# One level of Strassen's algorithm in the first feed-forward product of a fused encoder layer

## The chip, the core and the metric

The kernel runs as one program on one core of a Trainium2 chip. TensorE (PE) multiplies matrices into PSUM banks; VectorE (DVE), ScalarE (ACT) and GpSimd (POOL) work elementwise; SyncE (SP) issues this kernel's DMAs. Each engine works through its own list of instructions in order, and an instruction may wait for semaphores that other engines and the DMAs raise. The metric is the time of one execution in microseconds (us) on the device.

## The reference

One layer for 2048 prompt tokens and 8 x 16 tokens of running streams, 2176 in all, model width 1024, in float32. Cut to what matters here:

```
h = rms_norm(x, norm_mix_w) * (1 + sc1) + sh1
u, z, xbc, dt = split(h @ w_in)              # input projection
ya = pool_mixer(u); yb = ssd_mixer(z, xbc, dt)
x = x + g1 * (concat(ya, yb) @ w_out)        # output projection
h = rms_norm(x, norm_ffn_w) * (1 + sc2) + sh2
f = square(relu(h @ w_ff1 + b_ff1)) @ w_ff2 + b_ff2   # 1024 -> 4096 -> 1024
x = x + g2 * f
y = rms_norm(x, final_norm_w)
```

The two feed-forward products, `h @ w_ff1` and `(...) @ w_ff2`, are equally large. The shift, scale and gate vectors (sh, sc, g) are one set for the prompt and one for each of the 8 streams.

## The kernel before, in words

**Numbers.** Activations lie transposed: 128 features on the partitions, tokens along the free axis. To keep float32 precision every operand is split into a high part (a cast to `fp32r`) and a low part (the value minus the high part). `mm3` (L173) multiplies high by high, high by low and low by high: three matmuls for each 128x128 weight tile (a k-tile), added in one PSUM bank. `wsplit` (L163) loads 512 KB of weights into `wr`, makes the high part `wh` on ScalarE (L168) and the low part `wl` on VectorE (L170).

**Blocks and phases.** The tokens are cut into five blocks of 384 and one of 256 (`TBS`; the last holds the 128 tokens of the running streams). Blocks are worked on in three pairs (`SUPERS`), so that each weight tile serves two blocks. Phase A (input projection and the two mixers) comes first, then phase O (`out_proj`, L814), then the feed-forward (L968 to L982). Between phases, results go through DRAM: `yD` and `pD` hold the mixers' outputs, `xD` the stream after the output projection. The last write of `yD` is at L640, by a DMA on SyncE's queue.

**Feed-forward.** `load_r` (L838) reads a pair's `xD` tiles, keeps them as the residual input `xs`, and sums their squares for the norm. `load_h` (L860) scales them by the norm's factor and the modulation (`modulate`) and splits them: 2 blocks x 8 k-tiles, each with two instructions on VectorE and two on ScalarE. `ff1` (L881) makes four weight tiles of 128 outputs at a time: for each tile and block 8 k-tiles, so 24 matmuls, into one PSUM bank; then ReLU (L895) and the square's high part (L896) on ScalarE, the square (L897) and its low part (L898) on VectorE. `ff2` (L902) multiplies these by the second weights, 12 matmuls for each output tile, and adds the result to `xs` (L913). Per pair, `ff1` and `ff2` alternate eight times, with `ff1` one step ahead. The last `ff2` of a pair sums squares, normalizes and writes the output (L943).

**What sets the order.** Each engine's list is drawn up when the kernel is built, from the order of the program text, moved by `tc.high_priority(offset=...)`, and by when buffers come free: a tile of a pool with a fixed number of buffers waits for the last user of its buffer. Side work (the loading of the next inputs) is kept in a list of steps, `fill`; `filler(n)` takes n of them at chosen places, `drain()` takes all. Large activations lie in three classes of buffers, `c0`, `c1` and `c2` (`qt`), of 32 tiles each; a class passes from one phase's use to the next's. PSUM gives four banks `g`, two `y` and two `t`; `obank` deals out `g` and `y` in turn.

## Time and profile before

| | |
|---|---|
| Median of three runs | 2984.9 us (2980.18 to 2986.68) |
| Span of the profiled execution | 2982.6 us |
| TensorE busy | 2920.5 us, 98% |
| VectorE busy | 1812.6 us, 61% |
| ScalarE busy | 1170.2 us, 39% |
| GpSimd busy | 0.2 us |
| Read from and written to DRAM | 292.53 MB and 49.08 MB, 115 GB/s over the span |

The span runs from the first instruction to the last of one execution that the hardware profiler took. A busy time is the time in which at least one instruction of the engine was under way. A matmul's own duration in the profile is longer than the distance from its start to the next one's start, since matmuls overlap; where TensorE is never idle, the length of a stretch divided by its number of matmuls is the time that one takes up.

### The profile page before, as it was taken

The page shows a single profiled execution, that of the slowest core. Times are in us where ns is not written, and L with a number is a line of the kernel's source. Part 1 is how long each engine was busy: PE and PEld are TensorE (multiplying, and loading weights), DVE is VectorE, ACT ScalarE, POOL GpSimd, SP SyncE. Part 2 cuts the span into 40 slices and gives each one's busy share as a digit, 9 for nine tenths or more (in the row PEclk, how much of TensorE's full clock was granted, in tenths as well). Part 3 has the DMA queues.
Part 4 walks back from the last instruction along what each step waited for, and adds up shares of the span by engine and source line. Part 5 has one row for each costly group of instructions (what it writes and reads, how often), then busy time and mean ns, then how long its engine had stood idle before and what let it go on. Part 6 is the DMA issues. An engine that isn't in the chain of part 4 may idle for free.

```text
span 2982.6 us, 44472 instructions
## 1 busy us (share of the span) xinstructions
PE 2920.5 (98%) x17572; PEld 2822.1 (95%) x17572; DVE 1812.6 (61%) x3592; ACT 1170.2 (39%) x2098; POOL 0.2 (0%) x4
## 2 busy tenths in 40 slices
PE   7999999999999999999999999999999999999998
PEld 5889998989989899999999999999999999999997
DVE  8588796778978684543644444674444458445546
ACT  7646455544624233232622222542222234332232
POOL 0000000000000000000000000000000000000000
PEclk8999999999999999999999999999999999999999
DMA  6657343523564565563111111141111113222122
GB/s 233 195 181 218 130 127 111 149 91 114 160 166 150 157 204 168 144 220 123 62 64 64 64 64 64 63 163 64 64 64 64 57 64 135 75 75 78 71 78 78
DMA packets 218433, 344.51 MB, mean 116 GB/s; under 512 B 48816, under 2 KB 163440, under 8 KB 218224
## 3 DMA queue, kind: packets, MB, share of 16 engines
q1 hardware_dynamic: 218224, 341.67, 35.9%
q8 instruction: 138, 2.26, 0.3%
q14 instruction: 71, 0.58, 0.1%
HBM read 292.53 MB, written 49.08 MB: 115 GB/s over the span
## 4 chain that ended last, share of the span: by engine, by line
PE 90%; DVE 4%; DMA 4%; ACT 1%; issue 1%; SPq 0%; DVEq 0%; ACTq 0%
PE g L174 20%; PE g L175 20%; PE g L176 20%; PE y L176 7%; PE y L175 7%; PE y L174 7%; PE y L591 1%; PE t L596 1%; PE y L589 1%; DMA sb<-h 1%; PE t L254 1%; PE t L231 1%; DMA E<-aD 1%; PE g L211 1%; DMA EA<-aD 1%
## 5 line engine op out<-in xcount | busy, mean ns | idle before, releaser
L174 PE MATMUL g<-h,wh 128*128 128x384 f32 (+1 forms) x2584 | 856.5, 332 | 7.2 <-ACT h L785 3.5
L176 PE MATMUL g<-h,wl 128*128 128x384 f32 (+1 forms) x2584 | 857.8, 332 | 0.0
L175 PE MATMUL g<-h,wh 128*128 128x384 f32 (+1 forms) x2584 | 855.4, 331 | 0.0
L168 ACT CAST wh<-wr 128x1024 fp32r<-128x1024 f32 x386 | 403.1, 1050 | 987.7 <-PE g L175 740.8
L170 DVE TENSOR_TENSOR wl<-wr,wh 128x1024 fp32r<-128x1024 f32 x386 | 470.9, 1224 | 361.6 <-ACT wh L168 352.0
L174 PEld LDWEIGHTS g<-h,wh 128*128 128x128 f32 x2584 | 489.7, 190 | 19.2 <-issue 7.8
L175 PEld LDWEIGHTS g<-h,wh 128*128 128x128 f32 x2584 | 489.6, 189 | 9.5 <-issue 6.8
L176 PEld LDWEIGHTS g<-h,wl 128*128 128x128 f32 x2584 | 489.7, 190 | 8.7 <-issue 5.9
L174 PE MATMUL g<-c,wh 128*128 128x384 f32 (+1 forms) x1300 | 428.8, 330 | 1.4 <-ACT c L785 1.4
L176 PE MATMUL g<-c,wl 128*128 128x384 f32 (+1 forms) x1300 | 428.6, 330 | 0.0
L175 PE MATMUL g<-c,wh 128*128 128x384 f32 (+1 forms) x1300 | 428.1, 329 | 0.0
L913 DVE SCALAR_TENSOR_TENSOR c<-g,mod,c 128x384 f32<-128x384 f32 (+1 forms) x261 | 150.3, 576 | 199.2 <-PE g L176 198.8
L174 PEld LDWEIGHTS g<-c,wh 128*128 128x128 f32 x1300 | 244.3, 188 | 2.9 <-ACT c L785 2.2
L175 PEld LDWEIGHTS g<-c,wh 128*128 128x128 f32 x1300 | 244.2, 188 | 0.4
L176 PEld LDWEIGHTS g<-c,wl 128*128 128x128 f32 x1300 | 244.1, 188 | 0.4
L897 DVE TENSOR_TENSOR m<-m 128x384 f32<-128x384 f32 x192 | 102.3, 533 | 211.5 <-ACT c L896 211.5
L176 PE MATMUL y<-h,wl 128*128 128x384 f32 (+1 forms) x680 | 223.7, 329 | 0.0
L175 PE MATMUL y<-h,wh 128*128 128x384 f32 (+1 forms) x680 | 223.7, 329 | 0.0
L174 PE MATMUL y<-h,wh 128*128 128x384 f32 (+1 forms) x680 | 223.6, 329 | 0.0
L175 PE MATMUL y<-c,wh 128*128 128x384 f32 (+1 forms) x620 | 202.8, 327 | 0.0
L176 PE MATMUL y<-c,wl 128*128 128x384 f32 (+1 forms) x620 | 202.8, 327 | 0.0
L174 PE MATMUL y<-c,wh 128*128 128x384 f32 (+1 forms) x620 | 202.7, 327 | 0.0
(219 smaller groups left out, 3529.6 us busy)
## 6 DMA issues: line engine op xcount, KB each, us to landing
wr<-wf SPq DMA_DIRECT2D x204, 512.0 KB, 3.5
wr<-win SPq DMA_DIRECT2D x84, 512.0 KB, 4.2
wr<-wada SPq DMA_DIRECT2D x48, 512.0 KB, 5.0
E<-aD SPq DMA_DIRECT2D x34, 512.0 KB, 5.6
x<-xT SPq DMA_DIRECT2D x88, 192.0 KB, 3.1
wr<-wob SPq DMA_DIRECT2D x24, 512.0 KB, 3.9
wr<-wcD SPq DMA_DIRECT2D x24, 512.0 KB, 3.5
x<-uD SPq DMA_DIRECT2D x40, 199.5 KB, 3.3
```

The costliest lines, as they stand in the source:

```text
L168: S.copy(wh, raw)
L170: V.tensor_tensor(wl, raw, wh.bitcast(F32), op=ALU.subtract)
L174: T_.matmul(out, lhsT=wh, rhs=ah, start=start, stop=False)
L175: T_.matmul(out, lhsT=wh, rhs=al, start=False, stop=False)
L176: T_.matmul(out, lhsT=wl, rhs=ah, start=False, stop=stop)
L211: T_.matmul(out, lhsT=csh[i][:, k, :], rhs=wh[:, k2 * 512:(k2 + 1) * 512], start=(i + k == 0), stop=False)
L231: T_.matmul(pn[:, c:c + 1], lhsT=acc[:, c * P:(c + 1) * P], rhs=ones[:, 0:1], start=True, stop=True)
L254: T_.matmul(pr[:, :T], lhsT=ones, rhs=dg[:, :T], start=True, stop=True)
L589: T_.matmul(pO[:, pr, :], lhsT=St[g][:, pr * P:(pr + 1) * P], rhs=Cg, start=True, stop=True)
L591: T_.matmul(pD[64 * (h % 2):64 * (h % 2) + 64, h // 2, :], lhsT=xdt[:, h, :], rhs=M[:, h, :], start=True, stop=True)
L897: V.tensor_tensor(t, t, t, op=ALU.mult)
L913: V.scalar_tensor_tensor(x1[:, :Tp], pg[:, :Tp], G[:, 0:1], x1[:, :Tp], op0=ALU.mult, op1=ALU.add)
```

## The change

**The product.** `ff1` gives way to `ff1_unit`. A unit takes two weight tiles of 128 outputs (m0 = 2u, m1 = 2u + 1), the two halves of the contraction (512 each) and the pair's two token blocks, and sees them as a 2 x 2 by 2 x 2 product of blocks. One level of Strassen's algorithm, in Winograd's form, makes it with 7 block products in place of 8: each is 4 k-tiles, so 12 matmuls, and a pair has 16 units. Three of the four PSUM banks (`pa`, `pc`, `pb`) take a second product on top of the first (`more=True`): what the first left is read before, or counts in the sum. Further sums of results are made by VectorE on the way out (L995 to L997, L1004, L1006) in tiles `e` of a new pool `fe` with six buffers. `put` then makes ReLU, square and high part on ScalarE in three instructions and the low part on VectorE.

**Operands.** Strassen's products need four sums of weight blocks (s1 to s4) and four sums of activations (t1 to t4). The weight sums are made once for all pairs by GpSimd, in `combine`, 32 times (16 units, two halves): two DMAs bring 256 KB each into the single buffer `pp`, four additions of 128 x 256 follow, and a DMA writes 512 KB to a scratch `sD[u]` in DRAM; all three DMAs are issued by GpSimd. `combine` is called after the loads of the first pair's mixer outputs and ahead of the first `out_proj`. `wpair` then loads pairs of 512-column pieces, from the weights or from `sD`, and splits them. The activation sums are made by VectorE in `load_h`, which now reads the `xD` tiles itself through staging tiles, scales them (`affine`) and gives seven operands for each quarter: b11, t3 and t1 in class `c2`, t2, b21, t4 and b22 in `c1`. `load_x` reads the residual input again.

**Blocks and order.** The feed-forward's blocks become four of 364 and two of 360 tokens (`FBS`), since both blocks of a pair must be equally wide; the columns sum to 2176 in both. `xcols` gathers a block of 364 or 360 from the `xD` blocks of 384. `rsqrt_diag` takes widths that are no multiple of 128. `ff2(i)` needs the units 2i and 2i + 1 and runs after unit 2i + 2; the last two follow unit 15. The pool `pp` is closed ahead of the feed-forward, and `fe` takes over its memory. Cut from the diff below are changes of comments, the passing on of arguments, and the functions told in words.

```diff
+FBS = [364, 364, 364, 364, 360, 360]
...
     def rsqrt_diag(tp, acc, T, scale, epsval):
-        n = T // P
+        n = -(-T // P)
+        if T < n * P:
+            V.memset(acc[:, T:n * P], 1.0)
...
+    def affine(t, xk, r, dim, Ac, Bc):
+        T, _, last, Tp = dim
         V.tensor_tensor(t, xk, r[:, :T], op=ALU.mult)
         S.activation(t[:, :Tp], t[:, :Tp], AF.Identity, scale=Ac[:, 0:1], bias=Bc[:, 0:1])
...
+    sD = [dr.tile([P, 4, 512], F32, name=f"sD{u}") for u in range(16)]
+
+    def combine(pool, u, half):
+        hs = slice(256 * half, 256 * half + 256)
+        w = pool.tile([P, 4, 256], F32, tag="pp", name="pp", bufs=1)
+        for i in range(2):
+            nc.gpsimd.dma_start(w[:, 2 * i:2 * i + 2], a["wf1"][2 * u + i].rearrange("p (b x) -> p b x", b=2)[:, :, hs])
+        for out, x, y, op in ((3, 2, 3, ALU.add), (2, 0, 2, ALU.subtract), (0, 3, 0, ALU.subtract), (1, 1, 0, ALU.subtract)):
+            nc.gpsimd.tensor_tensor(w[:, out], w[:, x], w[:, y], op=op)
+        nc.gpsimd.dma_start(sD[u][:, :, hs], w)
+
+    def xcols(dst, k, t0, T):
+        for s, (lo, n) in enumerate(zip(OFFS, TBS)):
+            b, e = max(t0, lo), min(t0 + T, lo + n)
+            if b < e:
+                DQ.dma_start(dst[:, b - t0:e - t0], xD[s][k][:, b - lo:e - lo])
...
+    def load_h(sup, rs):
+        T = FBS[sup[0]]
+        hs = {n: [None] * 4 for n in HOPS}
+
+        def put(n, q, raw):
+            cls = "c2" if n in ("b11", "t3", "t1") else "c1"
+            hi, lo = qt(cls, F32R), qt(cls, F32R)
+            S.copy(hi[:, :T], raw)
+            V.tensor_tensor(lo[:, :T], raw, hi[:, :T].bitcast(F32), op=ALU.subtract)
+            hs[n][q] = (hi, lo)
...
+        def one(q):
+            b11, b12, b21, b22 = raws(q)
+            put("b11", q, b11)
+            t1 = tmp()[:, :T]
+            V.tensor_tensor(t1, b12, b11, op=ALU.subtract)
+            V.tensor_tensor(b12, b22, b12, op=ALU.subtract)
+            put("t3", q, b12)
+            put("t1", q, t1)
+            V.tensor_tensor(t1, b22, t1, op=ALU.subtract)
+            put("t2", q, t1)
+            put("b21", q, b21)
+            V.tensor_tensor(t1, b21, t1, op=ALU.subtract)
+            put("t4", q, t1)
+            put("b22", q, b22)
...
-    def ff1(sup, hs, i, cls):
...
+    def ff1_unit(sup, hs, u, cls):
...
+        def put(j, q, c):
+            fh, fl = qt(cls, F32R), qt(cls, F32R)
+            S.activation(c, c, AF.Relu)
+            S.activation(c, c, AF.Square)
+            S.copy(fh[:, :T], c)
+            V.tensor_tensor(fl[:, :T], c, fh[:, :T].bitcast(F32), op=ALU.subtract)
+            f[j][q] = (fh, fl)
...
+        pa, pc, pb, pd = (bank(ps, "g", GB) for _ in range(4))
+        wa11, ws3 = wpair(a11, s3_)
+        prod(pa, wa11, "b11")
+        c11 = ev()
+        S.activation(c11, pa[:, :T], AF.Identity, bias=VC("bf1", m0))
+        prod(pc, ws3, "t3")
+        ws1, ws2 = wpair(s1, s2)
+        prod(pb, ws1, "t1")
+        prod(pa, ws2, "t2", True)
+        u2 = ev()
+        S.copy(u2, pa[:, :T])
+        wa12, wa22 = wpair(a12, a22)
+        prod(pd, wa12, "b21")
+        v = ev()
+        V.tensor_tensor(v, u2, pc[:, :T], op=ALU.add)
+        V.scalar_tensor_tensor(v, pb[:, :T], VC("bf1", m1), v, op0=ALU.add, op1=ALU.add)
+        V.tensor_tensor(c11, c11, pd[:, :T], op=ALU.add)
+        prod(pc, wa22, "t4", True)
+        ws4, = wpair(s4)
+        prod(pb, ws4, "b22", True)
+        put(0, 0, c11)
+        put(1, 1, v)
+        c21 = ev()
+        V.scalar_tensor_tensor(c21, pc[:, :T], VC("bf1", m1), u2, op0=ALU.add, op1=ALU.add)
+        put(0, 1, c21)
+        V.scalar_tensor_tensor(u2, pb[:, :T], VC("bf1", m0), u2, op0=ALU.add, op1=ALU.add)
+        put(1, 0, u2)
...
+    pstack = ExitStack()
+    pp = pstack.enter_context(tc.tile_pool(name="pp", bufs=1))
+    for u in range(16):
+        for half in range(2):
+            combine(pp, u, half)
     pin1 = in_pool(SUPERS[1], "c2")
...
     with tc.high_priority(offset=FPRIO):
-        filler(16)
+        drain()
+    pstack.close()
+    fe = region("fe")
...
+        for u in range(16):
+            f[u] = ff1_unit(sup, hs, u, "c1" if u == 15 else "c0")
+            if u >= 2 and u % 2 == 0 and u < 14 or u == 15:
+                for i in ([u // 2 - 1] if u < 15 else [6, 7]):
...
+                    ff2(sup, xs, i, fi, i == 7)
```

**What moves.** On GpSimd nothing ran before but a few settings at the program's start. Now its list goes on with the rounds of `combine`. The names in brackets are the semaphores waited for: DMAHW are the DMA queues of SyncE, DMASW those of GpSimd, the rest are engines.

```order
L857 DMA pp<-wf 128x2x256 [waits DMAHW3_49,DMAHW2_49,DMAHW4_49,DMAHW1_49,DMAHW5_49,DMAHW0_49,DMAHW6_49,DVE_49,DMAHW7_49,PE_49,Activation_49]
L857 DMA pp<-wf 128x2x256
L859 ISA
L859 TENSOR_TENSOR pp<-pp 128x256 [waits DMASW1_49]
L859 TENSOR_TENSOR pp<-pp 128x256 [waits DMASW0_49,Pool_49]
L859 TENSOR_TENSOR pp<-pp 128x256 [waits Pool_49] x2
L860 DMA sD_10895<-pp 512x1x256 [waits Pool_49]
L857 DMA pp<-wf 128x2x256 [waits DMASW2_49]
```

The first load waits for all that has gone before on the other engines and SyncE's queues; the load of the second round waits for the write of the first.

On ScalarE at the start of the feed-forward, before (L286, L290 and L873 are `load_h`, L895 and L896 the first evictions of `ff1`, L168 a weight split):

```order
L290 CAST h<-m 128x384 [waits Activation_49]
L873 ACTIVATE c_13717<-c_13717,g2b 128x384
L290 CAST h<-m 128x384 [waits Activation_49]
L286 ACTIVATE m<-m,mod,A_89 128x384 [waits DVE_49]
L895 ACTIVATE m<-g,vec 128x384 [waits DVE_49,PE_49]
L290 CAST h<-m 128x384 [waits Activation_49]
L896 ACTIVATE c_14933<-m 128x384 [waits Activation_49]
L873 ACTIVATE c_13718<-c_13718,g2b 128x384
L873 ACTIVATE c_13719<-c_13719,g2b 128x384
L168 CAST wh<-wr 128x1024 [waits DMAHW7_49,PE_49]
```

The same place after (L295 and L899 are `load_h`, L985 is the first unit's first eviction into a tile `e`):

```order
L295 ACTIVATE x<-x,mod,A_89 128x364 [waits DVE_49,Activation_49]
L899 CAST c_15233<-x 128x364 [waits DVE_49]
L899 CAST c_15237<-m 128x364
L899 CAST c_15277<-x 128x364 [waits Activation_49]
L295 ACTIVATE x<-x,mod,A_89 128x364 [waits DMAHW7_49,DMAHW0_49,DVE_49]
L985 ACTIVATE e<-g,vec 128x364 [waits DMASW3_49,DMASW4_49,DMASW2_49,DMASW5_49,DMASW1_49,DMASW6_49,DMASW0_49,DMASW7_49,PE_49,Pool_49]
L899 CAST h<-m 128x364 [waits DVE_49]
L295 ACTIVATE x<-x,mod,A_89 128x364 [waits DVE_49]
L899 CAST h<-x 128x364
```

The first eviction now names every DMA queue of GpSimd and GpSimd itself among its waits, and the rest of `load_h` stands behind it.

On VectorE in the middle of the first pair, before (L897 and L898 belong to `ff1`, L913 to `ff2`):

```order
L170 TENSOR_TENSOR wl<-wr,wh 128x1024
L897 TENSOR_TENSOR m<-m 128x384
L898 TENSOR_TENSOR c_15770<-m,c_15769 128x384
L897 TENSOR_TENSOR m<-m 128x384
L898 TENSOR_TENSOR c_15764<-m,c_15763 128x384
L170 TENSOR_TENSOR wl<-wr,wh 128x1024
L897 TENSOR_TENSOR m<-m 128x384
L913 SCALAR_TENSOR_TENSOR c_13711<-g,mod,c_13711 128x384
L898 TENSOR_TENSOR c_15772<-m,c_15771 128x384
L913 SCALAR_TENSOR_TENSOR c_13719<-y,mod,c_13719 128x384
L913 SCALAR_TENSOR_TENSOR c_13712<-g,mod,c_13712 128x384
L913 SCALAR_TENSOR_TENSOR c_13720<-g,mod,c_13720 128x384
```

The same work after, in one unit (L954 is `wpair`, L995 to L997, L1004 and L1006 the sums of results, L975 the low parts):

```order
L954 TENSOR_TENSOR wl<-wr,wh 128x1024
L954 TENSOR_TENSOR wl<-wr,wh 128x512
L954 TENSOR_TENSOR wl<-wr,wh 128x1024
L995 TENSOR_TENSOR e<-e,g 128x364
L997 TENSOR_TENSOR e<-e,g 128x364
L996 SCALAR_TENSOR_TENSOR e<-g,vec,e 128x364
L1004 SCALAR_TENSOR_TENSOR e<-g,vec,e 128x364
L975 TENSOR_TENSOR c_17288<-e,c_17287 128x364
L954 TENSOR_TENSOR wl<-wr,wh 128x1024
L1006 SCALAR_TENSOR_TENSOR e<-g,vec,e 128x364
L975 TENSOR_TENSOR c_17294<-e,c_17293 128x364
L954 TENSOR_TENSOR wl<-wr,wh 128x1024
```

Between two weight splits there were up to four short instructions; in a unit the sums of results and the low parts come together in its second half, with weight splits among them.

## Rows read from the trace of the kernel before

**Rows 1.** The page: span, busy time by engine, the chain by engine.
```profile
span 2982.6 us, 44472 instructions
...
PE 2920.5 (98%) x17572; PEld 2822.1 (95%) x17572; DVE 1812.6 (61%) x3592; ACT 1170.2 (39%) x2098; POOL 0.2 (0%) x4
...
PE 90%; DVE 4%; DMA 4%; ACT 1%; issue 1%; SPq 0%; DVEq 0%; ACTq 0%
```

**Rows 2.** Busy time by stretch (x: instructions), then granted clock, DMA share, GB/s.
```profile
core 0: us, PE busy (x) PEld busy (x) DVE busy (x) ACT busy (x) POOL busy (x), PEclk, DMA share, GB/s
1052.00:1424.00 372.00, 370.12 (x2237) 368.24 (x2235) 189.79 (x364) 123.11 (x199) 0.00 (x0) 1.00 0.54 168
1424.00:1452.00 28.00, 25.07 (x131) 23.92 (x132) 24.06 (x51) 26.89 (x53) 0.00 (x0) 0.94 0.15 52
1500.00:1800.00 300.00, 300.00 (x1718) 300.00 (x1717) 125.56 (x180) 71.72 (x100) 0.00 (x0) 1.00 0.18 63
2550.00:2850.00 300.00, 300.00 (x2042) 300.00 (x2041) 151.08 (x293) 87.30 (x134) 0.00 (x0) 1.00 0.22 76
1875.00:1955.00 80.00, 80.00 (x460) 79.74 (x459) 55.40 (x93) 47.92 (x82) 0.00 (x0) 1.00 0.22 76
```

**Rows 3.** SyncE's queue in time order, 1046 to 1049 us: start, duration, issue.
```profile
1048.17 0.37 SPq L640 DMA_DIRECT2D yD<-zz  x1
```

**Rows 4.** ScalarE in time order, 1423.5 to 1424.5 us.
```profile
1424.00 0.45 ACT L830 ACTIVATE m<-y,g1b,mod 128x128 f32<-128x128 f32 x1
```

**Rows 5.** VectorE's groups by form: count, busy us, mean ns, idle before.
```profile
L170 DVE TENSOR_TENSOR wl<-wr,wh 128x1024 fp32r<-128x1024 f32 x386 | 470.9, 1224 | 361.6 <-ACT wh L168 352.0 <-PE g L212 3.0 <-DMA wr<-wada 1.4
L913 DVE SCALAR_TENSOR_TENSOR c<-g,mod,c 128x384 f32<-128x384 f32 x221 | 136.3, 617 | 171.2 <-PE g L176 170.8
L897 DVE TENSOR_TENSOR m<-m 128x384 f32<-128x384 f32 x160 | 88.9, 556 | 211.5 <-ACT c L896 211.5
...
L897 DVE TENSOR_TENSOR m<-m 128x256 f32<-128x256 f32 x32 | 13.4, 419 | 0.0
```

**Rows 6.** DMA issues: count, KB each, median us from issue to landing.
```profile
wr<-wf SPq DMA_DIRECT2D x204, 512.0 KB, 3.5
...
E<-aD SPq DMA_DIRECT2D x34, 512.0 KB, 5.6
...
yD<-zz SPq DMA_DIRECT2D x10, 768.0 KB, 4.1
...
zz<-xT SPq DMA_DIRECT2D x2, 768.0 KB, 8.4
```

**Rows 7.** VectorE's largest group by form from 1052 to 1424 us.
```profile
L170 DVE TENSOR_TENSOR wl<-wr,wh 128x1024 fp32r<-128x1024 f32 x46 | 56.3, 1224 | 79.0 <-ACT wh L168 79.0
```

**Rows 8.** ScalarE's groups by form.
```profile
L168 ACT CAST wh<-wr 128x1024 fp32r<-128x1024 f32 x386 | 403.1, 1050 | 987.7 <-PE g L175 740.8 <-PE y L175 232.5 <-PE g L211 8.1
L896 ACT ACTIVATE c<-m 128x384 fp32r<-128x384 f32 x160 | 84.2, 526 | 4.7
L895 ACT ACTIVATE m<-g,vec 128x384 f32<-128x384 f32 x99 | 57.2, 578 | 112.6 <-PE g L176 112.6
...
L290 ACT CAST h<-m 128x384 fp32r<-128x384 f32 x40 | 20.0, 499 | 0.0
```

**Rows 9.** VectorE in time order, 2975 to 2983 us.
```profile
2975.95 3.22 DVE L943 SCALAR_TENSOR_TENSOR c<-c,vec,t 128x256 f32<-128x256 f32 x8 [1.38 <-PE t L254]
```

More of the change, by code (lines that the diff above doesn't have):

```diff
@@ L31 @@
 TM = max(TBS)
+FBS = [364, 364, 364, 364, 360, 360]
+FOFFS = [sum(FBS[:i]) for i in range(len(FBS))]
+FLAST = len(FBS) - 1
+FLP = FBS[FLAST] - NB * DS
 _V = {}
@@ L171, in wsplit, with mm3 @@
         return wh, wl
-    def mm3(out, wh, wl, ah, al, start, stop):
-        T_.matmul(out, lhsT=wh, rhs=ah, start=start, stop=False)
-        T_.matmul(out, lhsT=wh, rhs=al, start=False, stop=False)
-        T_.matmul(out, lhsT=wl, rhs=ah, start=False, stop=stop)
+    def mm3(out, wh, wl, ah, al, start, stop, more=False):
+        T_.matmul(out, lhsT=wh, rhs=ah, start=start, stop=False, skip_group_check=more)
+        T_.matmul(out, lhsT=wh, rhs=al, start=False, stop=False, skip_group_check=more)
+        T_.matmul(out, lhsT=wl, rhs=ah, start=False, stop=stop, skip_group_check=more)
     csw = ca.tile([P, KT, 192], F32R, name="cs")
@@ L276, in s3, with fdims @@
         return ap.rearrange("p (b i) -> p b i", b=NB)
+    def fdims(s):
+        T = FBS[s]
+        return T, FOFFS[s], s == FLAST, (FLP if s == FLAST else T)
     def dims(s):
@@ new lines, in load_x, with wpair @@
+        return xs
+    def wpair(*srcs):
+        n = 512 * len(srcs)
+        with tc.high_priority(offset=WPRIO):
+            raw = wp.tile([P, 1024], F32, tag="wr", name="wr", bufs=WRB)
+            for i, src in enumerate(srcs):
+                DQ.dma_start(raw[:, 512 * i:512 * i + 512], src)
+            wh = wp.tile([P, 1024], F32R, tag="wh", name="wh")
+            S.copy(wh[:, :n], raw[:, :n])
+            wl = wp.tile([P, 1024], F32R, tag="wl", name="wl")
+            V.tensor_tensor(wl[:, :n], raw[:, :n], wh[:, :n].bitcast(F32), op=ALU.subtract)
+        return [(wh[:, 512 * i:512 * i + 512], wl[:, 512 * i:512 * i + 512]) for i in range(len(srcs))]
@@ new lines, in ff1_unit, with prod, ev @@
+    def ff1_unit(sup, hs, u, cls):
+        T = FBS[sup[0]]
+        m0, m1 = 2 * u, 2 * u + 1
+        def prod(out, w, n, more=False):
+            for q in range(4):
+                sl = slice(q * P, (q + 1) * P)
+                hi, lo = hs[n][q]
+                mm3(out[:, :T], w[0][:, sl], w[1][:, sl], hi[:, :T], lo[:, :T], q == 0 and not more, q == 3, more)
+        def ev():
+            return fe.tile([P, TM], F32, tag="e", name="e", bufs=6)[:, :T]
+        def put(j, q, c):
[5 more added lines that the diff above has]
+            f[j][q] = (fh, fl)
+        f = [[None] * 2 for _ in sup]
+        s2, s4, s3_, s1 = (sD[u][:, i] for i in range(4))
+        a11, a12, a22 = a["wf1"][m0][:, 0:512], a["wf1"][m0][:, 512:], a["wf1"][m1][:, 512:]
+        pa, pc, pb, pd = (bank(ps, "g", GB) for _ in range(4))
[25 more added lines that the diff above has]
+        put(1, 0, u2)
@@ L905, in tile_m @@
             mm = m % 2
-            T, t0, last, Tp = dims(s)
+            T, t0, last, Tp = fdims(s)
             x1 = xs[j][m]
```

100 lines of the change are left out of this document (43 added, 57 removed).

## The prediction

> **What bounds the kernel now.** I read the page's busy shares and chain first. TensorE (PE) is busy 98% of 2982.6 us and carries 90% of the chain; GpSimd (POOL) has 4 instructions in all [rows 1]. The reader is to see that only TensorE's time counts, unless another engine makes it wait. The table by stretches says how tightly. From 1500 to 1800 us, feed-forward on blocks of 384, TensorE is never idle, at full granted clock (2.4 GHz), with 1718 matmuls: 300/1718 = 174.6 ns each. From 2550 to 2850 us, blocks of 384 and 256 in equal number, 2042 matmuls take 146.9 ns each, so one of 256 columns takes 2 x 146.9 - 174.6 = 119.2 ns [rows 2]. The difference, 55.4 ns over 128 columns, is 0.433 ns a column. VectorE is busy 42% and ScalarE 24% of the first of these stretches. The groups by form and the DMA list then give the price of what is added.
>
> **The product itself.** The first product runs, for a pair of blocks, 32 weight tiles x 2 blocks x 24 matmuls = 1536; the change runs 16 units x 7 products x 12 = 1344. The second stays at 1536. By the slope a matmul of 364 columns takes 174.6 - 20 x 0.433 = 165.9 ns, one of 360 takes 164.2. Before: 1536 x (5 x 174.6 + 119.2) = 1524 us for the three pairs, both products. After: 1344 x (165.9 + 165.9 + 164.2) = 667 us and 1536 x 496.0 = 762 us, together 1429. **Saved: 95 us.** All of it is on the path. The new block widths alone change nothing: the columns sum to 2176 in both.
>
> **The GpSimd chain, the term that decides.** GpSimd forms the four weight sums of each unit: 32 times two DMAs in (512 KB together), four dependent additions of 128x256, one DMA out (512 KB). There is one buffer, so each round starts when the last one's output has landed. By the order the first waits for the last write of yD in the SSD phase, issued at 1048.2 us [rows 3], with 4 us to land: 1052. The end is awaited too: the pool "e" of the first eviction takes the chain's place in memory, and by the order that eviction, on ScalarE, waits for GpSimd's last rounds. Behind it on ScalarE stand the remaining third of load_h and the next weight casts, so TensorE runs dry within a few products.
>
> When would that eviction be ready otherwise? The output projection's last eviction starts on ScalarE at 1424.0 [rows 4]. In the order 58 VectorE instructions of load_h follow, 36 of them ahead of this eviction. At 0.42 us (256 columns) to 0.556 us (384) each [rows 5] the 58 take 24 to 32 us, I take 28; 36 of them make 17, so 1442. The chain has 390 us, 12.2 us a round.
>
> The trace has no GpSimd addition and no DMA issued by it, so a round is bounded by the nearest rows. Below: 3.5 us to load 512 KB, four additions at VectorE's 0.42 for 256 columns, and 4.1 us for the write of 768 KB [rows 5, 6]: 9.3 us. Above: 8.4 us, the slowest large load, each way [rows 6], and four additions at VectorE's 1.22 for 1024 columns [rows 5]: 21.7 us. I take 12.5: 4.6 in (midway between the 3.5 and the 5.6 of two loads of 512 KB, whose memory rows are longer and shorter than the 1 KB here), 4.5 out (a little over 4.1, as other transfers run beside it) and 0.85 an addition (midway between 0.42 and 1.22). Then 32 rounds make 400 us, the chain ends at 1452, **10 us late**. Every us on a round is 32 us.
>
> VectorE is busy 190 of the 372 us in which the chain runs, 56 of it in weight splits, which read two tiles of on-chip memory [rows 2, 7]. The Trainium skill (SBUF — State Buffer, Who interferes with whom) says that a VectorE instruction with two SBUF inputs and a GpSimd instruction that reads SBUF lock each other out, the second waiting for the whole of the first. By that rule each addition waits part of a VectorE instruction about every second time, an estimate of 0.2 us, near 1 us a round; no row of before can show it. The skill's DMA: Bandwidth & Descriptors (Anatomy of one DMA — SWDGE path) gives about 2.0 us plus bytes at 436 GB/s for a DMA from GpSimd: 3.2 us for 512 KB each way, an estimate of 9.8 us a round with my additions, by which the chain would be in time and the sum 10 us better. The two pull apart; the sum goes by the rows.
>
> **The start of the feed-forward.** Before, load_h needed two VectorE instructions a tile; now a quarter of the contraction needs 15 (4 scalings, 4 differences, 7 low parts). Half its tiles share the class c1 with the output projection's inputs, so by the order nearly all of it stands behind the projection's end. In these 28 us the order gives TensorE about 60 matmuls of the first unit, 10 us of work: 18 us idle. Before, 131 matmuls ran in the 28 us from 1424, where 28/0.1746 = 160 fit: 5 us lost, with the clock at 0.94 [rows 2]. I add 2 us for a lower clock after the longer gap. **Cost 15 us**, between 5 and 25.
>
> **Inside a unit.** At the end of the fourth product (t2) ScalarE may cast the next unit's first weights (1.05 us), then VectorE subtracts (1.22 us) [rows 5, 8]: 2.27 us. TensorE needs them after 12 + 2 matmuls, 2.32 us. Nothing is spare; I take 0.15 us for each of 48 units, **7 us** (0 to 30). The banks suffice: by the order each is evicted a product or more before it is needed again. Load does not bind in the mean: two units and one second product last 59 us on TensorE, against which ScalarE has 28 casts and activations at about 0.5 us and 11 weight tiles at 1.05 (26 us), VectorE 34 evictions and subtractions at about 0.55 and 11 tiles at 1.22 (32 us) [rows 5, 8].
>
> **Between the pairs.** While the last unit and the last two second products run (78 us of TensorE), VectorE has load_h (60 instructions), 32 evictions, 12 weight tiles, 14 additions of squares and the unit's own work: by durations 32 + 20 + 15 + 8 + 9 = 84 us, by the spacing when they follow each other some 70. Before, the same place had 55 of 80 us [rows 2]. I take 5 us for each of two such places, **10 us** (0 to 30).
>
> **Rest.** The output projection runs beside the chain's 33 MB, 84 GB/s on top of 168; the DMA share would rise from 0.54 to 0.81 [rows 2]. TensorE is busy 370 of 372 us there, covered by weights and inputs loaded ahead; if that cover thins, transfers at the two changes of input are late: 3 us (0 to 15). The last block is 360 wide, not 256: the eight closing multiplications took 3.22 us [rows 9], now about 4.5, with four shorter steps 2 us (1 to 4).
>
> **Sum.** 95 - 10 - 15 - 7 - 10 - 3 - 2 = 48 us. The profiled execution has a span of 2982.6 us; the median of the runs is 2984.9, so 2.3 lie around it, which I leave. 2984.9 - 48 = **2937 us**.
>
> **Rivals.**
> The first ends on the other side: the chain is much later. Mechanism: GpSimd's rounds, each with a full wait for two transfers and the additions held up beside a busy VectorE. With all else as above 58 us are gained without it, so it decides from 1442 + 58 = 1500 on, which is (1500 - 1052)/32 = 14.0 us a round. At 15 us a round the time is 2984.9 - 58 + 90 = 3017 us, at 17 us 3081. For it: nothing hides a round, the DMA share is high, and VectorE is half busy. Against it: the nearest rows make 9.3 us.
> The second: everything is hidden. The chain is in time (12 us or less) and the start, the units and the pairs cost half: 95 - 8 - 4 - 5 - 4 = 74, so 2911 us. For it: VectorE idles more than half of the steady stretch. Against it: the order puts load_h behind the projection's end.
> The third: the units bind. ScalarE and VectorE serve TensorE in order, four banks are all taken, and each unit loses 0.7 us more: 48 x 0.7 = 34, so about 2970 us. For it: the 2.27 against 2.32 us; against it: the second product between units lets queues catch up.
> The fourth: the change does not do what it says, as matmuls of 364 columns take the time of 384. Then FF takes 3 x (1344 + 1536) x 0.1746 = 1509 us, only 15 are saved and the time is about 3017 us. The straight line between 256 and 384 columns speaks against it.
>
> **How the numbers follow.** The forecast (chain up to 35 us late, others near their values): 0.50. Second rival 0.13, third 0.10, first 0.24, fourth 0.03. Faster by over 0.2% (about 6 us, what a measurement here can tell from no change): forecast, second and third, less 0.03 for those near the line, 0.70; slower 0.26, taking one hundredth of the first as even; within 0.2%: 0.04. The range reaches from 2903, below the second rival, to 3012, a round of 14.8 us. The forecast's own range is 2915 to 2965.
>
> **What would show it.** Right: 3 x (1536 - 1344) = 576 fewer matmuls, those of 364 columns spaced 166 ns; GpSimd's last addition near 1445 to 1455 us and TensorE idle for some 25 us around 1425 to 1460. Wrong: rounds longer than 14 us, so that ScalarE's first "e" waits for GpSimd beyond 1500; idle TensorE of more than half a microsecond in each unit, released by VectorE's wl or by evictions; a spacing of 364 columns above 170 ns.

## The result, and the profile after

The changed kernel takes 3002.4 us (median of five runs, 2994.8 to 3009.0) against 2982.9 us of the kernel before (five runs): a ratio of 1.0064, interval 1.0047 to 1.0082. It is slower by about 19 us where 48 us less were forecast. What came is in the main the first rival: the chain of weight sums ended at 1513.7 us, past the 1500 from which that rival decides. The profiled execution is the slowest of the five.

The page of the changed kernel, the lines that answer to [rows 1]:

```profile
span 3007.2 us, 45269 instructions
...
PE 2859.1 (95%) x17000; PEld 2742.3 (91%) x17000; DVE 1969.7 (65%) x3832; ACT 1348.3 (45%) x2518; POOL 184.2 (6%) x228
...
PE 73%; DMA 9%; issue 6%; POOL 5%; DVE 4%; ACT 2%; SPq 0%; DVEq 0%; POOLq 0%; ACTq 0%
```

TensorE has 572 matmuls and 61 us of work less than before, but its idle time grew from 62 to 148 us, and the chain that ended last now runs 9% through DMAs and 5% through GpSimd. The busy times by stretch, columns as in [rows 2]:

```profile
core 0: us, PE busy (x) PEld busy (x) DVE busy (x) ACT busy (x) POOL busy (x), PEclk, DMA share, GB/s
1424.00:1515.00 91.00, 21.59 (x97) 17.63 (x96) 27.79 (x48) 22.93 (x43) 37.34 (x49) 0.56 0.46 147
1515.00:1560.00 45.00, 41.99 (x219) 39.34 (x218) 31.96 (x55) 35.92 (x73) 0.00 (x0) 0.91 0.66 193
1600.00:1850.00 250.00, 250.00 (x1495) 247.78 (x1494) 136.46 (x215) 104.19 (x183) 0.00 (x0) 1.00 0.31 101
2600.00:2900.00 300.00, 300.00 (x1817) 297.68 (x1817) 170.95 (x314) 118.70 (x204) 0.00 (x0) 1.00 0.29 97
1930.00:2050.00 120.00, 113.41 (x656) 111.09 (x656) 99.53 (x191) 75.54 (x142) 0.00 (x0) 0.97 0.58 180
```

The third and fourth rows are the steady feed-forward: TensorE never idle, 167.2 ns a matmul on blocks of 364 (250/1495) and 165.1 with 360 (300/1817). The first two are where the time went: in 91 us after the output projection TensorE works for 21.6, at a mean granted clock of 0.56 (mostly the lower level, 1.2 GHz), and 45 us more pass before it is back at full pace. What it waited for from 1424 us on (total, times, longest):

```profile
PE g L178 <- ACT e L985: 47.6, 1, 47.6
PE g L178 <- ACT c L899: 15.9, 3, 8.8
```

One wait of 47.6 us, and its releaser is the first eviction of `ff1_unit`. On ScalarE, where [rows 4] stood, in time order:

```profile
1464.62 0.69 ACT L295 ACTIVATE x<-x,mod,A 128x364 f32<-128x364 f32 x1 [0.26 <-DVE x L294]
1513.78 0.56 ACT L985 ACTIVATE e<-g,vec 128x364 f32<-128x364 f32 x1 [48.47 <-DMA sD<-pp]
```

ScalarE was free at 1465.2, when the instruction ahead of the eviction was done, and TensorE's last matmul ahead of the gap started at 1466.3; the eviction started at 1513.8. So up to 48.5 us went to a write of `sD` that has nothing to do with the eviction but the memory. GpSimd in time order, with one round in full, its successor's start and the last:

```profile
1058.49 1.57 POOL L857 DMA_DIRECT2D pp<-wf  x2 [1058.05 <-issue]
...
1072.94 1.43 POOL L857 DMA_DIRECT2D pp<-wf  x2 [4.34 <-DMA sD<-pp]
1079.65 4.46 POOL L859 TENSOR_TENSOR pp<-pp 128x256 f32<-128x256 f32 x4 [5.28 <-DMA pp<-wf]
1084.52 0.76 POOL L860 DMA_DIRECT2D sD<-pp  x1 [0.41 <-POOL pp L859]
1088.85 1.42 POOL L857 DMA_DIRECT2D pp<-wf  x2 [3.57 <-DMA sD<-pp]
...
1510.32 0.76 POOL L860 DMA_DIRECT2D sD<-pp  x1 [0.41 <-POOL pp L859]
```

The groups of GpSimd while the output projection runs (1058 to 1424 us), 25 rounds:

```profile
L859 POOL TENSOR_TENSOR pp<-pp 128x256 f32<-128x256 f32 x100 | 92.1, 921 | 109.5 <-DMA pp<-wf 103.6
L857 POOL DMA_DIRECT2D pp<-wf x50 | 35.7, 721 | 1154.4 <-issue 1058.0 <-DMA sD<-pp 96.3
L860 POOL DMA_DIRECT2D sD<-pp x25 | 18.9, 758 | 10.2 <-POOL pp L859 10.2
```

A round is, in us: 1.43 for GpSimd to issue two loads (35.7/25), 4.14 of waiting for them (103.6/25), 3.68 for four additions (92.1/25), 0.41 and 0.76 until the write is issued (10.2/25, 18.9/25), and 4.0 of waiting for the write (96.3/24): 14.4. Over all 32 it is (1513.7 - 1058.5)/32 = 14.2.

### The profile page after: what moved, and what is told of

Its sections match the earlier page's. It is cut to its first block, busy times and chain, and to the rows that moved or that the text cites. A ratio compares the mean times of both kernels' runs of the same rounds, so it can differ in the third digit from the quotient of the medians.

```text
span 3007.2 us, 45269 instructions
## 1 busy us (share of the span) xinstructions
PE 2859.1 (95%) x17000; PEld 2742.3 (91%) x17000; DVE 1969.7 (65%) x3832; ACT 1348.3 (45%) x2518; POOL 184.2 (6%) x228
## 4 chain that ended last, share of the span: by engine, by line
PE 73%; DMA 9%; issue 6%; POOL 5%; DVE 4%; ACT 2%; SPq 0%; DVEq 0%; POOLq 0%; ACTq 0%
PE g L180 19%; PE g L178 19%; PE g L179 19%; DMA sD<-pp 4%; POOL pp L859 4%; PE y L180 3%; PE y L178 3%; PE y L179 3%; POOL pp L857 2%; PE y L604 1%; PE t L609 1%; PE y L602 1%; DMA sb<-h 1%; PE t L260 1%; PE t L237 1%
## 5 line engine op out<-in xcount | busy, mean ns | idle before, releaser
L178 PE MATMUL g<-h,wh 128*128 128x384 f32 (+3 forms) x2432 | 814.2, 335 | 56.0 <-ACT e L985 47.6
L179 PE MATMUL g<-h,wh 128*128 128x384 f32 (+3 forms) x2432 | 812.6, 334 | 1.8 <-DVE h L900 1.6
L180 PE MATMUL g<-h,wl 128*128 128x384 f32 (+3 forms) x2432 | 814.0, 335 | 0.0
L178 PE MATMUL g<-c,wh 128*128 128x364 f32 (+3 forms) x1792 | 592.4, 331 | 26.0 <-ACT c L899 15.9
L180 PE MATMUL g<-c,wl 128*128 128x364 f32 (+3 forms) x1792 | 593.7, 331 | 0.8 <-DVE wl L174 0.6
L179 PE MATMUL g<-c,wh 128*128 128x364 f32 (+3 forms) x1792 | 591.1, 330 | 2.3 <-DVE c L900 2.0
L178 PEld LDWEIGHTS g<-c,wh 128*128 128x128 f32 x1792 | 339.4, 189 | 30.2 <-ACT c L899 17.2
L180 PEld LDWEIGHTS g<-c,wl 128*128 128x128 f32 x1792 | 339.2, 189 | 8.8 <-DVE wl L954 4.9
L179 PEld LDWEIGHTS g<-c,wh 128*128 128x128 f32 x1792 | 339.2, 189 | 3.9 <-DVE c L900 2.9
L954 DVE TENSOR_TENSOR wl<-wr,wh 128x1024 fp32r<-128x1024 f32 x192 | 209.5, 1091 | 154.3 <-ACT wh L952 150.7
L1021 DVE SCALAR_TENSOR_TENSOR c<-g,mod,c 128x364 f32<-128x364 f32 (+2 forms) x256 | 146.0, 571 | 170.9 <-PE g L180 170.6
L178 PE MATMUL y<-c,wh 128*128 128x364 f32 (+3 forms) x608 | 200.2, 329 | 3.1 <-DVE c L1021 3.1
L180 PE MATMUL y<-c,wl 128*128 128x364 f32 (+3 forms) x608 | 200.4, 330 | 1.3 <-DVE wl L174 1.3
L179 PE MATMUL y<-c,wh 128*128 128x364 f32 (+3 forms) x608 | 199.8, 329 | 0.0
L972 ACT ACTIVATE e<-e 128x364 f32<-128x364 f32 (+1 forms) x192 | 95.1, 496 | 77.3 <-DVE e L997 72.4
```

The costliest lines, as they stand in the source:

```text
L178: T_.matmul(out, lhsT=wh, rhs=ah, start=start, stop=False, skip_group_check=more)
L179: T_.matmul(out, lhsT=wh, rhs=al, start=False, stop=False, skip_group_check=more)
L180: T_.matmul(out, lhsT=wl, rhs=ah, start=False, stop=stop, skip_group_check=more)
L954: V.tensor_tensor(wl[:, :n], raw[:, :n], wh[:, :n].bitcast(F32), op=ALU.subtract)
L972: S.activation(c, c, AF.Relu)
L1021: V.scalar_tensor_tensor(x1[:, :Tp], pg[:, :Tp], G[:, 0:1], x1[:, :Tp], op0=ALU.mult, op1=ALU.add)
```

## The experiments

"Projection" in the table is the time from SyncE's issue of the last write of yD [rows 3] to the last matmul of 256 columns; it was 374.7 us in the kernel before. "Eviction" is the start of the first eviction into `e`, counted from that matmul. "Chain" is GpSimd's last issue of a write to sD. These three come from the one profiled execution of each run. It lies within 7 us of the median, but for chain early (the fastest of ten, 18 us below) and long rounds (11 us above).

| run | median us | of before (interval) | projection | chain | eviction |
|---|---|---|---|---|---|
| changed kernel | 3002.4 | 1.0064 (1.0047 to 1.0082) | 377.0 | 1510 | 82.4 |
| two buffers | 2970.3 | 0.9941 (0.9921 to 0.9961) | 397.0 | 1385 | 26.5 |
| memory apart | 2975.1 | 0.9947 (0.9931 to 0.9964) | 379.5 | 1525 | 38.8 |
| no sums | 2945.0 | 0.9852 (0.9837 to 0.9866) | 373.4 | none | 26.9 |
| no additions | 2959.1 (one run) | 0.990 | 379.3 | 1418 | 29.3 |
| sums by VectorE | 3050.1 | 1.0210 (1.0186 to 1.0234) | 474.8 | 1329 | 27.1 |
| the same, prepared | 3032.4 | 1.0153 (1.0138 to 1.0169) | 478.1 | 1329 | 8.2 |
| apart, prepared | 2961.9 | 0.9916 (0.9898 to 0.9933) | 396.7 | 1538 | 8.7 |
| two buffers, prepared | 2952.8 | 0.9889 (0.9874 to 0.9904) | 397.9 | 1381 | 9.1 |
| three loads | 3005.0 | 1.0068 (1.0047 to 1.0088) | 379.5 | 1500 | 69.6 |
| chain early | 2983.5 | 0.9990 (0.9973 to 1.0007) | 375.9 | early | 8.4 |
| two buffers, no additions | 2963.2 | 0.9919 (0.9894 to 0.9945) | 386.2 | 1319 | 26.9 |
| long rounds | 2991.3 | 1.0008 (0.9989 to 1.0027) | 417.8 | 1362 | 26.7 |

**Two buffers.**

```diff
-        w = pool.tile([P, 4, 256], F32, tag="pp", name="pp", bufs=1)
+        w = pool.tile([P, 4, 256], F32, tag="pp", name="pp", bufs=2)
```

> The weight sums get two buffers in place of one. Theory (the chain's rounds are too long because every step of a round waits for the one before, and the 47.6 us at the first eviction are its price): the write of a round, 4.0 us of wait, now runs beside the next round; a round falls from 14.2 to about 10.4 us, the chain ends near 1391 us, the first eviction no longer waits for it, and the time falls by 48 to 55 us to 2947 to 2955. Rival A (the transfers and the additions are limited by what runs beside them): rounds stay above 12.7 us, the chain still ends after 1465 us, and the time stays above 2965. Rival B (the wait only covers the rest of load_h and the weight casts): the wait goes, but another of 25 us or more stands in its place, and the time stays above 2977.

The chain was over at 1385 us (its last write landed at 1391, 10.3 us a round) and the wait was gone, as the theory had it, but 15 to 23 us of the gain were missing, so that the time fell where rival A had put it, without rival A's long rounds: the output projection took 20 us longer than in the changed kernel. VectorE and GpSimd of this run, each in time order:

```profile
1101.97 2.11 DVE L174 TENSOR_TENSOR wl<-wr,wh 128x1024 fp32r<-128x1024 f32 x1
1104.01 1.09 DVE L799 TENSOR_TENSOR c<-m,c 128x384 fp32r<-128x384 f32 x1
...
1108.59 0.55 DVE L338 SCALAR_TENSOR_TENSOR m<-sw,x 128x384 f32<-128x384 f32 x1
1109.06 0.55 DVE L799 TENSOR_TENSOR c<-m,c 128x384 fp32r<-128x384 f32 x1
...
1111.41 1.21 DVE L174 TENSOR_TENSOR wl<-wr,wh 128x1024 fp32r<-128x1024 f32 x1
```

```profile
1102.17 4.56 POOL L859 TENSOR_TENSOR pp<-pp 128x256 f32<-128x256 f32 x4
1107.18 0.75 POOL L860 DMA_DIRECT2D sD<-pp  x1 [0.45 <-POOL pp L859]
1107.86 0.72 POOL L857 DMA_DIRECT2D pp<-wf  x1
```

Beside the four additions (1102.17 to 1106.73) VectorE's weight split takes 2.11 us and its subtraction of 384 columns 1.09; after 1107.18, while GpSimd only issues a transfer, the same kinds take 0.55 and 1.21, as in [rows 5]. So beside these additions VectorE's instructions take nearly twice their time. With two buffers the additions of two rounds follow each other, and weight splits come late. What TensorE waited for from 1075 to 1390 us (total, times, longest), the two largest sums:

```profile
PE y L180 <- DVE wl L174: 4.8, 2, 3.2
PE g L180 <- DVE wl L174: 4.0, 3, 3.0
```

The busy times of this stretch, columns as before:

```profile
1075.00:1390.00 315.00, 302.89 (x1730) 299.23 (x1730) 206.08 (x313) 97.07 (x157) 182.26 (x218) 0.98 0.84 261
```

The same stretch without sums:

```profile
1075.00:1390.00 315.00, 314.78 (x1880) 314.11 (x1879) 161.22 (x318) 98.94 (x160) 0.00 (x0) 1.00 0.55 163
```

150 matmuls fewer in the same time; TensorE idles 12 us, the mean granted clock is 0.98, and VectorE is busy for 206 us in place of 161.

**Memory apart.**

```diff
-WRB = 4
+WRB = 3
...
-    pstack = ExitStack()
-    pp = pstack.enter_context(tc.tile_pool(name="pp", bufs=1))
+    pp = ctx.enter_context(tc.tile_pool(name="pp", bufs=1))
...
-    pstack.close()
     fe = region("fe")
```

> The chain is left as it is (one buffer), but its buffer keeps its own memory, so that the pool e no longer takes its place; to make room the weight loads have three buffers instead of four. Theory: the chain still ends near 1514 us, but nobody waits for it there; the first eviction runs when its product is ready, near 1466 us, and the time falls as in the run with two buffers, to 2945 to 2960. Rival A (what costs is the chain's own load on the transfers and on VectorE at the start of the feed-forward): less than half of the 48 us comes back, 2978 or more. Rival B (a later unit then waits for its sums): a wait of TensorE for a weight cast fed from sD shows after 1466 us.

The chain ran on until 1525 us, and the eviction waited for its own product alone:

```profile
1478.92 0.56 ACT L985 ACTIVATE e<-g,vec 128x364 f32<-128x364 f32 x1 [2.29 <-PE g L180]
```

That shows the memory shared with `e` as the cause of the wait. The gain fell short of the theory's by 15 us or more: with the chain beside it, `load_h` makes the first eviction ready 38.8 us after the projection, against 26.9 without sums. In the traced run another 6 us lie ahead of the projection: the last write of yD came at 1060.6 us, against 1054.3 in the changed kernel, and no run tells why. Rival B did not show. The control for the buffer that was given up:

> The changed kernel with three buffers for weight loads in place of four, and nothing else: a control for the runs in which the chain's buffer has its own memory. Theory: 1.006 of before as the changed kernel, within 0.002. Rival (a load fewer ahead makes weight casts late): 1.010 or more, which would have hidden a part of what the run with its own memory won.

Within 0.0004 of the changed kernel (the edit is `WRB = 3` alone), so the buffer of the loads plays no part.

**No sums.**

```diff
-        for half in range(2):
+        for half in range(0):
             combine(pp, u, half)
...
-        s2, s4, s3_, s1 = (sD[u][:, i] for i in range(4))
+        s2, s4, s3_, s1 = (a["wf1"][2 * u + i // 2].rearrange("p (b x) -> p b x", b=2)[:, i % 2] for i in range(4))
```

> The weight sums are left out altogether: the first product reads plain pieces of the weights where it read sums, so GpSimd and its transfers have nothing to do. Theory: a chain that is in time costs nothing, so this run comes within 5 us of the run with two buffers, 2945 to 2955. Rival (the chain's 33 MB each way and its additions slow the output projection too): 2940 or less, with the output projection shorter by 5 us or more than in the changed kernel.

Strassen's product without its weight sums gains 44 us; the sums as they were made cost 63 us (1.0064 - 0.9852), the wait being 48 of them. The theory falls: a chain that is in time still costs 27 us (0.9941 - 0.9852). The rival missed its numbers too (2945.0 us, where it had 2940 or less, and a projection 3.6 us shorter than in the changed kernel, where it had 5), but its mechanism shows in the faster chain, which lengthens the projection by 24 us. (Its 33 MB are both ways together: 32 times 512 KB are 16.8 MB each way.)

**No additions**, with one buffer and with two (the loop over the four `tensor_tensor` is cut):

> Of the chain the additions are left out: it loads the weights and writes them to sD as they are. Theory (the profile's parts of a round are right: 3.7 us of additions, 0.4 us behind them, and some 10 us of issuing and waiting for transfers): rounds of 10 to 10.4 us, the chain ends near 1385 us and the first eviction does not wait for it; the time is near that of two buffers. Rival (the additions are slow only because they wait for transfers and VectorE, and the transfers are limited by the load beside them): rounds above 12 us.

> Two buffers and no additions: only the chain's transfers are left, and they come faster still. Theory (with two buffers it is the additions, 8 in a row beside VectorE, that make the weight splits late in the output projection): VectorE's instructions keep 0.55 and 1.22 us, the output projection loses 10 us at most against the run without sums, the time is 0.987 to 0.992 of before. Rival (the transfers, at twice the rate, cost the 25 us): 0.993 or more.

With one buffer a round took 11.3 us ((1420.9 - 1059.5)/32, from the first load's issue to the last write's landing), between theory and rival. VectorE's groups in this run, 1075 to 1390 us:

```profile
L174 DVE TENSOR_TENSOR wl<-wr,wh 128x1024 fp32r<-128x1024 f32 x38 | 46.4, 1223 | 51.9 <-ACT wh L172 51.8
L846 DVE TENSOR_TENSOR x<-x,m 128x384 f32<-128x384 f32 x37 | 20.4, 553 | 41.7 <-ACT m L843 38.7 <-DMA x<-xT 2.8
```

With the transfers but without additions VectorE is as fast as in [rows 5]; with additions the same two groups had means of 1332 and 800 ns in the run with two buffers. The projection lost 6 us (one buffer) and 13 us (two) to transfers alone, against 24 with two buffers and additions. How transfers cost time although VectorE's instructions are as fast as ever, the waits show. VectorE from 1050 to 1420 us (total, times, longest), first without sums, then with two buffers and no additions:

```profile
DVE sw L334 <- DMA x<-uD: 0.6, 2, 0.3
DVE sw L334 <- DMA x<-uD: 13.1, 8, 3.2
```

The pooling mixer's inputs (`uD`) came late beside the chain's transfers, VectorE waited for them in its list, and the weight splits stood behind: TensorE waited 7.2 us for two of them from 1075 to 1390 us. So of the 24 us perhaps half is the additions, half the transfers; that is an estimate, for without additions the transfers also came faster (the chain was over at 1319 us, not 1385). The theory of the second run had put 10 at most on the transfers. Its time, 0.9919, is within the theory's range, but does not tell the two runs apart (0.9941).

**Sums by VectorE** (two buffers; `V.tensor_tensor` in place of `nc.gpsimd.tensor_tensor`).

> As the run with two buffers, but VectorE makes the 128 additions of the weight sums; GpSimd only issues the chain's transfers. Theory (GpSimd's additions and VectorE's instructions hold each other up, which is why VectorE's 384-column instructions took up to 1.09 us beside them and TensorE waited for weight splits): VectorE gets 128 x 0.42 = 54 us of work more, its other instructions keep their 0.55 and 1.22 us, no wait for wl over 1 us is left in the output projection, and the time is 2955 to 2964 with before at 2988, 6 to 15 us less than with two buffers. Rival A (the chain's transfers are what slows the output projection): the time stays within 4 us of that with two buffers, 0.994 of before, though VectorE's durations are back. Rival B (VectorE now waits in its list for the chain's transfers, with weight splits behind): additions idle VectorE for 30 us or more and the time is above 2975.

Rival B. VectorE's other instructions kept their times, but its list waited for the chain's loads (total, times, longest):

```profile
DVE pp L859 <- DMA pp<-wf: 108.6, 20, 13.4
```

The weight splits stood behind these waits, and the projection took 100 us more than without sums. In this program a wait for a transfer on GpSimd holds up only the chain; the same wait on VectorE holds up the weight splits that TensorE needs next.

**Prepared inputs.** `load_h`'s scalings and sums are made earlier and kept in DRAM:

```diff
+            t1, t2, t4 = (tmp()[:, :T] for _ in range(3))
+            V.tensor_tensor(t1, b12, b11, op=ALU.subtract)
+            V.tensor_tensor(b12, b22, b12, op=ALU.subtract)
+            V.tensor_tensor(t2, b22, t1, op=ALU.subtract)
+            V.tensor_tensor(t4, b21, t2, op=ALU.subtract)
+            for n, r in zip(HOPS, (b11, b12, t1, t2, b21, t4, b22)):
+                DQ.dma_start(hD[sup[0] // 2][n][q], r)
...
-    rs = load_r(SUPERS[0])
+    prepare(SUPERS[0], load_r(SUPERS[0]))
+    load_h(SUPERS[0], HOPS[:3], hs)
     out_proj(SUPERS[2], pin2, yin2, range(8))
     drain()
-    hs = load_h(SUPERS[0], rs)
+    load_h(SUPERS[0], HOPS[3:], hs)
```

> On top of the sums by VectorE, the scaled inputs and their four sums are made earlier and kept in DRAM (for the first pair during the last output projection, for the others during the middle of the pair before); at the change of pair only a load, a cast and a low part are left for each of the 28 operands, and of the first pair the 12 operands of class c2 are ready before the output projection ends. Theory (at the start and between the pairs the 15 VectorE instructions of a quarter are what TensorE waits for): the start loses about 12 us in place of 27, each change of pair about 5 in place of 10, so 20 to 25 us less than the run with sums by VectorE, 2930 to 2945. Rival (the 31 MB of further transfers and the same VectorE work, now in the output projection, cost as much there): within 6 us of that run.

> The inputs and sums prepared earlier, now with GpSimd's additions, one buffer with memory of its own (no wait at the first eviction). Theory (18 us came from preparing, whatever makes the weight sums; and the work that is left at the start of the feed-forward is small, so the chain that still runs there hurts it less): 0.995 less 0.006 to 0.008 of before, about 2946 to 2955 with before at 2986. Rival (the gain of preparing only replaced waits that VectorE's additions had caused): 2965 or more.

> The same with two buffers in the old place. Theory: 0.994 less 0.006 to 0.008 of before, 2945 to 2952, and the output projection still loses some 25 us to it, as with two buffers alone. Rival: 2963 or more.

The eviction came 8 to 9 us after the projection in all three, with two buffers 17 us earlier than without preparing. The time fell by 18 us (sums by VectorE), 15 (two buffers, 0.0052) and 9 (apart, 0.0031, between theory and rival: there the projection grew by 17 us). With sums by VectorE that is a little under the theory, with two buffers the time is just above it. Most of the gain is at the start; a change of pair gained less than the theory's 5 us (with two buffers 679 matmuls in place of 661 in the 120 us from 1910 us, 3 us of work). Two buffers with prepared inputs is the fastest of the runs that make all the sums, 1.1% faster than the kernel before.

**Chain early.** As apart and prepared, but `combine` is called before the input projection:

> As the run with its own memory and prepared inputs, but the chain runs from the start of the program, beside the input projection, and is over long before the output projection. Theory (the chain's additions cost where VectorE has no slack, its transfers where loads are late; neither is free, but it depends on what stands beside): the output projection and the start of the feed-forward are as without sums; in the first 460 us, where VectorE is busy some 78%, 114 us of additions take up to 57 us of its time and TensorE loses 10 to 25 us; together 2937 to 2952, 0.984 to 0.989 of before. Rival A (hidden there): 2925 to 2935. Rival B (the start, bound by weight loads, loses more than the output projection did): above 2957.

Rival B, at 0.9990: the projection (375.9 us) is nearly as without a chain and the eviction (8.4) as in the other prepared runs, but the last write of yD came some 30 us later than in the changed kernel (1085 against 1054). That trace is of the fastest of ten runs, which spread from 2965 to 2996 us; where the others lost more, no trace shows.

**Long rounds.**

```diff
-        hs = slice(256 * half, 256 * half + 256)
-        w = pool.tile([P, 4, 256], F32, tag="pp", name="pp", bufs=1)
+        hs = slice(512 * half, 512 * half + 512)
+        w = pool.tile([P, 4, 512], F32, tag="pp", name="pp", bufs=1)
...
-        for half in range(2):
-            combine(pp, u, half)
+        combine(pp, u, 0)
```

> The chain with one buffer in 16 rounds of 512 columns in place of 32 of 256: the same bytes and additions, half as many transfers issued, waited for and written. Theory (of a round of 14.2 us the larger part is fixed: 2.2 us in which GpSimd issues three transfers, and waits for loads and writes that hardly grow with their size): a round takes 18 to 22 us, the chain ends between 1350 and 1410 us, before the first eviction is ready near 1465, and the time is 0.990 to 0.995 of before. Rival (the round is bytes and additions): 27 us or more a round, the chain still ends after 1490 us, and the time is above 1.002 of before.

The round was as the theory said, about 19 us (16 from 1063.6 us to the landing of the last write, issued at 1362.2), and the wait was gone. The time was between theory and rival: the projection took 41 us more than in the changed kernel, in a run 11 us above the median of its ten. The stretch from 1075 to 1390 us:

```profile
1075.00:1390.00 315.00, 287.51 (x1596) 284.34 (x1597) 196.35 (x301) 90.90 (x149) 113.92 (x106) 0.95 0.77 250
```

Nearly 300 matmuls fewer than without sums. GpSimd and VectorE of this run:

```profile
1087.66 6.06 POOL L859 TENSOR_TENSOR pp<-pp 128x512 f32<-128x512 f32 x4 [5.97 <-DMA pp<-wf]
1090.94 1.64 DVE L846 TENSOR_TENSOR x<-x,m 128x384 f32<-128x384 f32 x1
```

An instruction of 384 columns on VectorE, 0.55 us by itself, took up to 1.09 us beside additions of 256 columns and takes 1.64 beside these of 512 (1.5 us each): what it loses grows with the addition beside it. That this makes the projection so much longer than with two buffers is not shown; transfers run beside it too.

## Why the prediction was wrong

**The GpSimd chain: the step that failed, by its size.** The prediction took 12.5 us a round and 10 us late; it was 14.2 us and 48.5 late. It had named 14.0 us as the point from which the change loses, and the first rival with this mechanism. Against its three parts, in the 25 rounds above: from the first load's issue to the additions 4.6 forecast, 5.6 measured; additions 3.4 against 3.7; from the write's issue to the next round 4.5 against 4.8; and 0.4 between additions and write, for which it had no term. The transfers themselves, from issue to landing (medians), were not slower than the 4.6 and 4.5 taken for them:

```profile
pp<-wf POOLq DMA_DIRECT2D x64, 256.0 KB, 4.1
sD<-pp POOLq DMA_DIRECT2D x32, 512.0 KB, 3.9
```

These rows count from the start of the issue, as those of [rows 6] do. The larger part of what was missing lies between the transfers: the second load is issued only when GpSimd is done with the first issue (0.72 us), and GpSimd starts the write 0.4 us after the last addition. Over 32 rounds 1.7 us are 54 us. The chain also began 6 us later than forecast, for the last write of yD came later:

```profile
1054.31 0.37 SPq L653 DMA_DIRECT2D yD<-zz  x1
```

(In the runs with a chain after the input projection this write lay between 1050 and 1061 us; why, no run tells.) By the Trainium skill's rule (DMA: Bandwidth & Descriptors, Anatomy of one DMA — SWDGE path) the prediction had an estimate of 3.2 us for 512 KB each way and 9.8 us a round. The write of 512 KB took 3.9 us from issue to landing, and the time between the steps came on top. The measurement decides.

**The additions.** The Trainium skill (SBUF — State Buffer, Who interferes with whom) says that a VectorE instruction with two SBUF inputs and a GpSimd instruction that reads SBUF lock each other out. The traces agree: 0.55 becomes 1.09 us on VectorE, and 1.64 beside additions of 512 columns; an addition takes 0.92 us on average during the projection and 0.79 (22.1/28) after 1424 us, when VectorE has little to do. The prediction had counted the page's rule on GpSimd's side alone, where it is worth 0.13 us an addition, 13 us over the 100 of the projection. On VectorE's side it is more, 206 us of busy time in place of 161 from 1075 to 1390 us with two buffers, and it costs time as soon as the chain is made faster.

**The start.** Forecast was the first eviction 18 us after the projection, and 15 us of cost. It was ready after 33.9 us, and after 26.9 with no chain at all. VectorE in time order, rows from the projection's last matmul (1431.3 us) on:

```profile
1431.44 0.56 DVE L294 TENSOR_TENSOR x<-x,rb 128x364 f32<-128x364 f32 x1 [9.16 <-DMA c<-xD]
1435.65 1.23 DVE L954 TENSOR_TENSOR wl<-wr,wh 128x1024 fp32r<-128x1024 f32 x1 [2.65 <-ACT wh L952]
1444.85 0.54 DVE L294 TENSOR_TENSOR x<-x,rb 128x364 f32<-128x364 f32 x1 [2.11 <-DMA x<-xD]
1447.72 1.05 DVE L900 TENSOR_TENSOR h<-x,h 128x364 fp32r<-128x364 f32 x1
```

Of `load_h` 38 instructions run on VectorE in these 33.9 us, so the count of 36 was nearly right. What it lacked: `load_h` now loads its inputs itself, and its scalings wait 5.0 us for xD behind the projection's end (another wait of 9.2 ends with it); two weight splits stand in between, 2.5 us and 2.7 of waiting for a cast; and some nine instructions take about 1.05 us in place of 0.54 beside the chain's additions, 4 us more. Without sums the loads cost 2.8 us, the weight splits about as much as here, the additions nothing.

From the projection's end to 1560 us the changed kernel made 255 matmuls of the feed-forward in 128.7 us, 43 us of work: 86 lost, against 5 before and 25 more forecast for chain and start together. That is 56 us too much: 38 for the chain (48.5 late in place of 10) and 18 for the start itself (about 32 in place of 15).

**Between the pairs.** From 1930 to 2050 us 656 matmuls ran, some 110 us of work; before, none was lost at this place:

```profile
1900.00:2020.00 120.00, 119.79 (x684) 118.39 (x683) 89.39 (x164) 67.18 (x116) 0.00 (x0) 1.00 0.37 128
```

(684 at 174.6 ns make 119.4.) So 10 us at the first of two places (the second is much the same, 659 matmuls from 2440 to 2560 us), 5 were taken; VectorE was busy for 99.5 of these 120 us (89.4 before), and what TensorE waited for there were evictions, 4.6 us for VectorE's and 1.9 for ScalarE's. So the mechanism is the forecast one, at twice the size.

**Inside a unit** 7 us were taken for late weight splits. TensorE is never idle in the steady rows, so these did not show; but 167.2 ns are 1.3 above the straight line, 7 us over the 5760 matmuls of 364 columns, and 165.1 are 0.9 above it, 3 us over those of 360. That the term came out nearly right is luck. **The saving** is 95 us as forecast. No sums bears it out: from the projection's end on it is 40 us shorter than before in the traces, and 95 less 24 at its start, 20 at the pairs and 10 for the spacing make 41. **The projection** lost 2.3 us (3 forecast), because a chain with one buffer is slow enough. **The end** moved by less than 1 us (2 forecast).

**Together:** 48 forecast, less 56 at the start, less 10 between the pairs: 18 us slower. The traces of the two kernels bear that out from the last write of yD on, where the changed one takes 18.5 us more. Their spans differ by 24.6 us: the other 6.1 lie ahead of that write, in the phase of the input projection, whose work the change leaves as it is. The medians differ by 19.5 us, so part of the nearness to 18 is chance. The first rival is not the whole account either: a wait of 48.5 us alone is less than the 58 us that the rest was to gain, and the change loses only together with the longer start.

What stays open: how the 24 us that a faster chain costs the projection divide exactly between transfers and additions, why the input projection ends later in some runs, and why the runs with a chain spread further than those of before (in long rounds 2974 to 3003 us in ten runs, against 2983 to 2990 in thirteen of before).

## What to carry to other kernels

Work on an idle engine is not free when it is one long chain: count every step of a round, the engine's own time to issue its transfers and the time between steps too, multiply by the rounds, and look up who takes over its memory, for there its lateness becomes a wait. Then ask what its instructions do to the engine beside it and what its transfers do to the loads for which that engine waits; a faster chain moved the price from one wait into the stage beside it (48 us of wait became 20 to 41 us of projection in the traces). And when a step takes its inputs from DRAM anew, its loads belong to its time, not only its instructions.

## What the runs showed of the hardware

- GpSimd was occupied 0.72 us by issuing a load of 256 KB in pieces of 1 KB and 0.76 us by a write of 512 KB in such pieces; with rows of 4 KB and 8 KB it was 0.54 and 0.58 us (long rounds).
- An addition of two 128x256 tiles took GpSimd 0.79 us with VectorE quiet and 0.92 on average beside it; VectorE's instructions took up to twice their time beside it (0.55 to 1.09, 1.21 to 2.11), and 0.55 became 1.64 beside additions of 128x512.
- GpSimd's transfers alone left VectorE's durations as they were (1223 and 553 ns), but made it wait for loads (13.1 us for `uD`, against 0.6).
- Matmuls of 364 columns were spaced 167 ns and those of 360 164 to 165 ns.
